# Memory attention chunk by chunk, output weights loaded by half rows beside it, gated values weighed two steps behind their load

## The chip, the cores and the metric

The kernel runs on one core of one Trainium2 chip. The metric is the device time of one execution in microseconds (us); less is better. The core has TensorE (PE, with its weight loads as PEld), VectorE (DVE), ScalarE (ACT), GpSimd (POOL) and SyncE (SP), which here only issues DMAs.

## What is computed

One decoder layer on x of 2048 x 1024, with a memory of 256 tokens, all in float32. Cut to what matters:

```python
h    = rmsnorm(x, norm_g)
proj = h @ w_in                               # 1024 -> 3584: q | k | v (768 each) | qm (256) | gate (1024)
mix  = dilated_window_mixer(q, k, v)          # 12 heads in 3 groups; each group's output is scaled by its
                                              # share of the groups' softmax denominators (per head and row)
mo   = memory_attention(qm, rmsnorm(mem, mem_norm_g), w_mem_kv)   # 4 heads over 256 memory tokens
y    = concat([mix, mo]) * silu(gate)         # 2048 x 1024
x    = x + y @ w_out                          # w_out 1024 x 1024
return rmsnorm(x, final_norm_g)
```

## The kernel before

**Tiling.** x is held transposed and split in two float32r parts, `xH` and `xL` (high and rest), as 4 chunks of 512 rows by 8 tiles of 128 columns (`k`). A projection of 128 columns for one chunk is 24 matmuls (8 tiles, three products high*high, high*rest, rest*high; L140 to L142). `Rb` holds the rows' 1/rms, 512 columns a chunk.

**Stages.** First six passes (three groups by two head pairs) with four chunks each do the window attention. Then comes the memory stage: eight units, one for each head pair `pp` and chunk `c`, pp outside and c inside. A unit is `proj_q`, `proj_gate` (48 matmuls) and a `burst`: the scores of this unit (`mem_scores`, L448), and the values (L437) of the unit two before it. Between a unit's scores and its values lie, for each half of the unit: row maxima (DVE L453), exponentials (ACT L457), reciprocals (DVE L460), a scaling of four tiles (POOL L464), a 32x32-block transpose (DVE L329) and a turn through DRAM (`turn_tiles`: one DMA of 512 KB out, L332, four of 128 KB back, L338). `values` ends with the product with the gate (DVE L420) and the store of the gated chunk to `z_dr` (SP L429).

Last comes the output stage: for each chunk `c` four blocks (`out_block`) of 48 matmuls (L642 to L644), `y` of that chunk by the output weights, then residual, RMS norm and the store. The residual rows are loaded at the start of a block (L633).

**What is prepared beside it.** `shares` turns the softmax statistics (six transposes on PE, L551, copies by DVE, 24 small DMAs to `st_dr`), computes the groups' shares and stores them to `f_dr`. `load_wo(k)` loads one full row tile of the output weights (512 KB) into a buffer of tag `wh`, casts it into `woH` (ACT L598) and subtracts into `woL` (POOL L599); `woH` and `woL` lie over chunks 0 and 1 of `xH` and `xL`. `make_y(c, k)` loads the gated values from `z_dr` (256 KB, L612) and for k < 6 their shares from `f_dr` (two of 128 KB, L616), multiplies (POOL, for every third k DVE; L618), casts into `yH` (ACT L619) and subtracts into `yL` (DVE L620); `yH` and `yL` of an even chunk lie over chunk 2 of `xH` and `xL`, of an odd one over chunk 3. Its shares' buffer is `wraw` with two buffers, which `load_w` uses too.

**What sets the order.** The projections and output blocks are generators; `run` counts a slot at each `yield` (every six matmuls; four slots a projection, eight a unit, eight a block), and `at(n, f)` calls f n slots later. So slots put the side work into program order. The framework then places the instructions on each engine by its own plan of when their operands are ready, with program order as the priority, so an engine's order can differ from the program's. All DMAs go through SP's one queue, in order: a DMA that waits holds up those behind it. With the slot M in which the memory stage begins: `shares` begins at M+13, the loads of weights 19 at M+16, the eight `load_wo` stand at M+41 to M+59, the eight `make_y(0, k)` at M+56 to M+63, the first output block at M+64.

Of the kernel before, what the change touches and what calls it, by code (L numbers as in the profile page):

```python
# [34 lines left out]
def trunk_kernel(ctx, tc, xT, xrows, w_in, g_in, w_out, memT, mrows, g_mem, w_mem, g_fin, nbias, ident_in, out):  # L35
# [78 lines left out]
    def to_blocks(ap, g):  # L114

        if g == 0:
            return ap.rearrange("p (b r i) -> p r b i", b=4, r=16)
        if g == 1:
            return ap.rearrange("p (b j i) -> p j b i", b=4, j=4)
        return ap  # L120

    def from_proj(ap, g):

        if g == 0:
            return ap.rearrange("p (r b i) -> p r b i", r=16, b=4)
        if g == 1:
            return ap.rearrange("p (j b i) -> p j b i", j=4, b=4)
        return ap
# [277 lines left out]
    def values(st, g, pp, c):  # L406
        o = pbank(ps_o, "po")
        for half in st["halves"]:
            assert half.ready
            if g == 3:  # L410
                mem_values(o, st, pp, half)
                continue
            for b in half.blocks:
                ts = [t for t in range(2) if (b, t, 0) in half.at]
                for t in ts:
                    for h in range(2):
                        pe.matmul(o[h * HD:(h + 1) * HD, b * P:(b + 1) * P], st["v"][:, b + t, h * HD:(h + 1) * HD],
                                  half.turned(b, t, h), start=(t == ts[0]), stop=(t == 1))
        u = st["u"]
        v.tensor_tensor(from_proj(u, g), from_proj(u, g), to_blocks(o, g), op=ALU.mult)  # L420
        dst = z_dr[g][:, pp, :]
        if g == 0:
            sp.dma_start(dst.rearrange("p (r c n) -> p r c n", r=16, c=4)[:, :, c, :],
                         u.rearrange("p (r n) -> p r n", r=16))
        elif g == 1:
            sp.dma_start(dst.rearrange("p (j r n) -> p j r n", j=4, r=4)[:, :, c, :],
                         u.rearrange("p (j n) -> p j n", j=4))
        else:
            sp.dma_start(dst[:, c * CH:(c + 1) * CH], u)  # L429
# [66 lines left out]
    def memory_kv(st):  # L496
        gm = sb([P, NK], F32, "gm", 1)
        sp.dma_start(gm, g_mem)
        halves = [t.bitcast(F32).rearrange("p k n -> p (k n)").rearrange("p (k n) -> p k n", k=4) for t in w_tiles()]
        for i, m in enumerate(halves):  # L500
            sp.dma_start(m, memT[:, 4 * i:4 * i + 4, :])
        yield
        rm = sb([P, 2, P], F32, "rm", 1)
        r = spread(rm, st["squares"], 2)
        next(r)
        for i, m in enumerate(halves):
            for j in range(2):
                for k in range(2 * j, 2 * j + 2):
                    a.activation(m[:, k, :], m[:, k, :], AF.Copy, scale=gm[:, 4 * i + k:4 * i + k + 1])
                yield  # L510
        next(r)
        raws = []

        def load(i):
            for j in range(2):
                raw = sb([P, 4, P], F32, "wraw", 2) if j else tmp().rearrange("p (k n) -> p k n", k=4)
                sp.dma_start(raw, w_mem[i, :, 4 * j:4 * j + 4, :])
                raws.append(raw)

        load(0)  # L520
        yield
        yield
        st["kk"] = sb([P, 5 * P], F32, "kk", 2)
        for i in range(4):
            if i < 3:
                load(i + 1)
            if i == 2:
                for _ in range(5):
                    yield
            ps = pbank()[:, :NMEM]  # L530
            for j in range(2):
                for k in range(4):
                    pe.matmul(ps, raws[2 * i + j][:, k, :], halves[j][:, k, :], start=(j + k == 0), stop=(j + k == 4))
                yield
            t = st["kk"][:, i * NMEM:(i + 1) * NMEM] if i < 2 else tmp()[:, :NMEM]
            v.tensor_tensor(t.rearrange("p (b n) -> p b n", b=2), ps.rearrange("p (b n) -> p b n", b=2), rm, op=ALU.mult)
            if i < 2:
                continue
            yield
            if i == 2:  # L540
                vb = sb([P, 5, P], F32, "vb", 2).rearrange("p b n -> p (b n)")[:, :2 * NMEM]
                st["v"] = vb.rearrange("p (k n) -> p k n", k=2)
            shift_tiles(st["v"][:, :, (i - 2) * P:(i - 1) * P], t.rearrange("p (k n) -> p k n", k=2))
        yield


    def shares():
        for i, src in enumerate((nm_all, l_all)):
            for g in range(3):
                pt = pbank()  # L550
                pe.transpose(pt[:64, :P], src[:, g].rearrange("p h b -> p (h b)"), ident)  # L551
                t = sb([P, CH], F32, "wraw", 2)[:64, :P]
                v.tensor_copy(t, pt[:64, :P])
                for h in range(4):
                    dst = st_dr[2 * g + i, h]
                    s = t[16 * h:16 * h + 16, :]
                    if g == 2:
                        sp.dma_start(dst.rearrange("(r n) -> r n", r=16), s)
                    elif g == 1:
                        sp.dma_start(dst.rearrange("(j b i) -> b j i", j=4, b=16),  # L560
                                     s.rearrange("b (j i) -> b j i", j=4))
                    else:
                        sp.dma_start(dst.rearrange("(r b i) -> b r i", r=16, b=16),
                                     s.rearrange("b (r i) -> b r i", r=16))
            yield
        q = S // 32
        m = sb([P, 5 * P], F32, "kk", 2)[:, :6 * q].rearrange("p (s n) -> p s n", s=6)
        sp.dma_start(m, st_dr.rearrange("s h (b n) -> (h b) s n", n=q))
        for _ in range(4):
            yield  # L570
        f = sb([P, 5, P], F32, "vb", 2).rearrange("p b n -> p (b n)")[:, :4 * q]
        f = f.rearrange("p (s n) -> p s n", s=4)
        v.tensor_tensor(f[:, 3, :], m[:, 0, :], m[:, 2, :], op=ALU.min)
        v.tensor_tensor(f[:, 3, :], f[:, 3, :], m[:, 4, :], op=ALU.min)
# [17 lines left out]
    def row_tile(tag):  # L592
        return sb([P, NK, P], F32R, tag, 4).bitcast(F32).rearrange("p k n -> p (k n)")

    def load_wo(k):
        raw = row_tile("wh")
        sp.dma_start(raw, w_out[:, k, :])
        a.copy(woH[:, k, :], raw)  # L598
        gp.tensor_tensor(woL[:, k, :], raw, woH[:, k, :].bitcast(F32), op=ALU.subtract)  # L599

    staged = []

    def make_y(c, k):
        yH, yL = xH[:, 2 + c % 2, k, :], xL[:, 2 + c % 2, k, :]
        cs = slice(c * CH, (c + 1) * CH)
        if not staged:
            kk = sb([P, 5 * P], F32, "kk", 2)
            vb = sb([P, 5, P], F32, "vb", 2).rearrange("p b n -> p (b n)")
            spare = row_tile("wl")
            staged.extend([kk[:, :CH], vb[:, :CH], spare[:, :CH], spare[:, CH:]])  # L610
        t = staged[k % 4]
        sp.dma_start(t, z_dr[k // 2][:, k % 2, cs])  # L612
        if k < 6:
            f = sb([P, CH], F32, "wraw", 2)
            for h in range(2):
                sp.dma_start(f[h * HD:(h + 1) * HD, :],  # L616
                             f_dr[k // 2, 2 * (k % 2) + h:2 * (k % 2) + h + 1, cs].broadcast_to([HD, CH]))
            (v if k % 3 == 2 else gp).tensor_tensor(t, t, f, op=ALU.mult)  # L618
        a.copy(yH, t)  # L619
        v.tensor_tensor(yL, t, yH.bitcast(F32), op=ALU.subtract)  # L620

    outr = out.rearrange("(u r) d -> r u d", r=16)
    gfin = []
# [52 lines left out]
    def at(delay, fn):  # L676
        todo.setdefault(slot[0] + delay, []).append(fn)
# [45 lines left out]
    for idx, (g, pp) in enumerate(pairs):  # L723
# [55 lines left out]
            burst((st, g, pp, c), 1, nbs[0])  # L779
            prev = st  # L780
        ws = following
    at(12, lambda: steps(shares()))
    for pp in range(2):
        for c in range(NC):
            st = {}
            if pp == 1 and c >= 1:
                for i, k in enumerate(((0, 1, 2), (3, 4, 5), (6, 7))[c - 1]):
                    at(2 * i + 1, lambda k=k: load_wo(k))
            if pp == 1 and c == 3:
                for k in range(NK):  # L790
                    at(k, lambda k=k: make_y(0, k))
            run(proj_q(st, 3, c, ws[2 + 2 * pp]))
            run(proj_gate(st, 3, c, ws[1 + 2 * pp], "nb" if (4 * pp + c) % 3 == 1 else "u"))
            if pp == 0 and c == 1:
                ws.append(load_w(w_in[19]))
            burst((st, 3, pp, c), 2)
    for c in range(NC):
        for b in range(4):
            if c < NC - 1:
                at(3, lambda: (make_y(c + 1, 2 * b), make_y(c + 1, 2 * b + 1)))  # L800
            run(out_block(c, b))
            if c == 0 and b in (0, 2):
                burst()
# [62 lines left out]
```

## Time and profile before

| | us |
|---|---|
| median of 3 runs | 1015.41 (1009.09 to 1016.02) |
| the profiled execution | 1015.06 |
| its span in the trace | 1013.3 |
| PE busy in the span | 968.4 (96%) |
| DVE, ACT, POOL busy | 425.3, 324.3, 257.1 |
| DMA: moved, share of 16 engines | 134.30 MB, 42.7% |

How to read it: a busy PE says that matmuls are in flight, also at a lowered clock; so beside the busy time stands the clock that was granted, as a share of 2.4 GHz (1.00 is 2.4 GHz, 0.50 is 1.2 GHz). Matmuls overlap, so their mean duration is longer than the distance from one start to the next. The memory stage lies at about 657 to 785 us of the span, the output stage behind it.

### The profile page before, as it was taken

How to read it: one execution, taken by the hardware profiler on the slowest of the kernel's cores; microseconds unless marked ns; L12 is line 12 of the kernel's file. 1: busy time of each engine (PE TensorE's matmuls, PEld its weight loads, DVE VectorE, ACT ScalarE, POOL GpSimd, SP SyncE). 2: the span in 40 equal slices, each digit the busy share in tenths (PEclk: the TensorE clock that was granted, in tenths of full speed). 3: DMA queues.
4: the chain of work that ended last, by engine and by line, in shares of the span. 5: the costliest groups of instructions: out<-in, count | busy, mean ns of one | idle time of the engine just before them, and what ended most of it. 6: DMA issues, size and time to landing. Idle time of an engine off the chain costs nothing. (4 is left out here: it accounts for less than half of the span.)

```text
span 1013.3 us, 13854 instructions
## 1 busy us (share of the span) xinstructions
PE 968.4 (96%) x4836; PEld 761.8 (75%) x4836; DVE 425.3 (42%) x982; ACT 324.3 (32%) x984; POOL 257.1 (25%) x396
## 2 busy tenths in 40 slices
PE   7899999999999999999999999999999679899997
PEld 5688888887788888777777777777767357688886
DVE  7866333333343333333333344324544434455433
ACT  5756422232234222432232324232333321222111
POOL 4411500140014000411132112143366641112000
PEclk9899999999999999999999999999999689899999
DMA  5465411142124322432245335414655777788311
GB/s 194 152 198 177 146 64 62 53 146 71 60 94 148 103 83 84 140 105 83 87 132 156 115 95 165 138 50 105 187 158 177 220 223 215 240 238 220 125 63 62
DMA packets 100982, 135.18 MB, mean 133 GB/s; under 512 B 29744, under 2 KB 63792, under 8 KB 100912
## 3 DMA queue, kind: packets, MB, share of 16 engines
q1 hardware_dynamic: 100912, 134.30, 42.7%
q8 instruction: 38, 0.62, 0.3%
q14 instruction: 32, 0.26, 0.1%
HBM read 89.14 MB, written 45.12 MB: 132 GB/s over the span
## 5 line engine op out<-in xcount | busy, mean ns | idle before, releaser
L140 PE MATMUL pp<-xH,wh 128*128 128x512 f32 x896 | 361.7, 404 | 3.2 <-DVE kk L249 2.8
L142 PE MATMUL pp<-xH,wl 128*128 128x512 f32 x896 | 357.7, 399 | 2.1 <-DVE wl L78 2.1
L141 PE MATMUL pp<-xL,wh 128*128 128x512 f32 x896 | 357.8, 399 | 1.4 <-DVE xL L198 1.4
L140 PEld LDWEIGHTS pp<-xH,wh 128*128 128x128 f32 x896 | 169.9, 190 | 53.4 <-issue 9.4
L142 PEld LDWEIGHTS pp<-xH,wl 128*128 128x128 f32 x896 | 169.7, 189 | 46.2 <-DVE wl L78 4.1
L141 PEld LDWEIGHTS pp<-xL,wh 128*128 128x128 f32 x896 | 169.9, 190 | 42.5 <-DVE xL L198 2.6
L320 POOL COPY vb<-mid 32x128 f32<-32x128 f32 (+1 forms) x208 | 59.6, 287 | 255.8 <-DVE mid L317 247.6
L642 PE MATMUL pp<-xH 128*128 128x512 f32 (+1 forms) x264 | 105.9, 401 | 16.0 <-ACT xH L619 11.9
L320 ACT COPY vb<-mid 32x128 f32<-32x128 f32 (+1 forms) x208 | 60.7, 292 | 166.7 <-DVE mid L317 164.4
L78 POOL TENSOR_TENSOR wl<-wraw,wh 128x512 fp32r<-128x512 f32 x52 | 67.5, 1312 | 151.3 <-ACT wh L77 146.0
L643 PE MATMUL pp<-xL,xH 128*128 128x512 f32 (+1 forms) x264 | 104.6, 397 | 0.0
L644 PE MATMUL pp<-xH,xL 128*128 128x512 f32 (+1 forms) x264 | 103.1, 395 | 0.0
L374 ACT ACTIVATE p<-p,nm_all 128x128 f32<-128x128 f32 (+1 forms) x192 | 86.1, 450 | 39.3 <-DVE nm_all L373 26.9
L329 DVE STREAM_TRANSPOSE mid<-p 128x1024 f32<-128x1024 f32 (+1 forms) x56 | 66.9, 1194 | 53.6 <-DMA t_dr<-mid 30.9
L464 POOL TENSOR_SCALAR p<-p,sm 128x256 f32<-128x256 f32 x64 | 59.4, 945 | 62.4 <-DVE sm L460 32.7
L642 PEld LDWEIGHTS pp<-xH 128*128 128x128 f32 x264 | 51.6, 196 | 29.8 <-ACT xH L619 14.0
L306 DVE SCALAR_TENSOR_TENSOR tmp<-pp,Rb 128x512 f32<-128x512 f32 x32 | 22.1, 690 | 123.6 <-PE pp L142 123.5
L307 ACT ACTIVATE u<-tmp 128x512 f32<-128x512 f32 x29 | 18.3, 631 | 140.3 <-DVE tmp L306 138.8
L373 DVE CUSTOM_DVE_ANT_0 p<-ps,nb 128x128 f32<-128x128 f32 (+1 forms) x192 | 57.0, 361 | 8.0 <-PE ps L395 7.9
L644 PEld LDWEIGHTS pp<-xH,xL 128*128 128x128 f32 x264 | 51.9, 197 | 10.8 <-DVE xL L620 0.2
L643 PEld LDWEIGHTS pp<-xL,xH 128*128 128x128 f32 x264 | 51.8, 196 | 10.1
L77 ACT CAST wh<-wraw 128x512 fp32r<-128x512 f32 (+1 forms) x60 | 33.9, 587 | 64.7 <-DMA wraw<-in_w_in 36.1
(129 smaller groups left out, 818.4 us busy)
## 6 DMA issues: line engine op xcount, KB each, us to landing
t_dr<-mid SPq DMA_DIRECT2D x46, 512.0 KB, 3.0
p<-t_dr SPq DMA_DIRECT2D x184, 128.0 KB, 3.5
wraw<-in_w_in SPq DMA_DIRECT2D x56, 256.0 KB, 3.0
wh<-in_xrows SPq DMA_DIRECT2D x16, 512.0 KB, 5.1
out<-wh SPq DMA_DIRECT2D x15, 512.0 KB, 2.7
z_dr<-u SPq DMA_DIRECT2D x29, 256.0 KB, 2.4
wraw<-f_dr SPq DMA_DIRECT2D x48, 128.0 KB, 5.2
tmp<-in_xT SPq DMA_DIRECT2D x22, 256.0 KB, 3.9
```

What stands on the lines that cost most here:

```text
L78: on.tensor_tensor(wl, raw, wh.bitcast(F32), op=ALU.subtract)
L140: pe.matmul(ps, wh[:, k, :], xh, start=(k == 0), stop=False)
L141: pe.matmul(ps, wh[:, k, :], xl, start=False, stop=False)
L142: pe.matmul(ps, wl[:, k, :], xh, start=False, stop=(k == NK - 1))
L320: (gp.tensor_copy if (i + j) % 2 else a.copy)(dst[32 * j:32 * j + 32, :, 32 * i:32 * i + 32], mid[32 * i:32 * i + 32, :, 32 * j:32 * j + 32])
L329: v.transpose(mid.rearrange("p (j t b) -> p t j b", j=4, t=n), src.rearrange("p (t j b) -> p t j b", t=n, j=4))
L373: v.tensor_tensor_reduce(p, sc, bias, -SCALE, BIG, ALU.add, ALU.min, nm)
L374: a.activation(p, p, AF.Exp, bias=nm, scale=-1.0, accum_out=l)
L464: gp.tensor_scalar(w, w, sm[:, 1, h, b:b + 1], None, op0=ALU.mult)
L642: pe.matmul(ps, yH[:, k, bs], woH[:, k, ns], start=(k == 0), stop=False)
L643: pe.matmul(ps, yH[:, k, bs], woL[:, k, ns], start=False, stop=False)
L644: pe.matmul(ps, yL[:, k, bs], woH[:, k, ns], start=False, stop=(k == NK - 1))
```

## The change

The eight units of the memory stage run in another order, (0,0), (0,1), (1,0), (1,1), (0,2), (1,2), (0,3), (1,3), so that chunks 0 and 1 are done with after four units. Then 16 half rows of the output weights (256 KB each) are loaded, one a slot from M+32, into four buffers (two in `Rb`, two of `wraw`), and each is split three slots after its load; every third subtraction goes to DVE. `make_y(0, k)` stands at M+52 to M+59, with four buffers for the values and three for the shares (partly in `Rb`), and its arithmetic (`finish`) is put two slots behind its loads; in the output stage the two `make_y` of a block stand at its slots 1 and 4, before both at 3. The store of the gated chunk is put two slots behind its product. `shares` begins at M+21 and keeps its copies in `vb` and `kk` rather than in `wraw`. Weights 19, which the third unit now needs at M+16, are loaded at M+13. No matmul is added or removed.

```diff
@@ -418,6 +418,9 @@
                                   half.turned(b, t, h), start=(t == ts[0]), stop=(t == 1))
         u = st["u"]
         v.tensor_tensor(from_proj(u, g), from_proj(u, g), to_blocks(o, g), op=ALU.mult)
+        at(2, lambda: store_z(u, g, pp, c))
+
+    def store_z(u, g, pp, c):
         dst = z_dr[g][:, pp, :]
         if g == 0:
             sp.dma_start(dst.rearrange("p (r c n) -> p r c n", r=16, c=4)[:, :, c, :],
@@ -542,14 +545,19 @@
                 st["v"] = vb.rearrange("p (k n) -> p k n", k=2)
             shift_tiles(st["v"][:, :, (i - 2) * P:(i - 1) * P], t.rearrange("p (k n) -> p k n", k=2))
         yield
+        yield
+        ws.append(load_w(w_in[19]))
+        yield
 
 
     def shares():
+        kk = sb([P, 5 * P], F32, "kk", 2)
+        vb = sb([P, 5, P], F32, "vb", 2)
         for i, src in enumerate((nm_all, l_all)):
             for g in range(3):
                 pt = pbank()
                 pe.transpose(pt[:64, :P], src[:, g].rearrange("p h b -> p (h b)"), ident)
-                t = sb([P, CH], F32, "wraw", 2)[:64, :P]
+                t = (vb[:64, 3 * i + g, :] if 3 * i + g < 5 else kk[:64, :P])
                 v.tensor_copy(t, pt[:64, :P])
                 for h in range(4):
                     dst = st_dr[2 * g + i, h]
@@ -564,11 +572,11 @@
                                      s.rearrange("b (r i) -> b r i", r=16))
             yield
         q = S // 32
-        m = sb([P, 5 * P], F32, "kk", 2)[:, :6 * q].rearrange("p (s n) -> p s n", s=6)
+        m = kk[:, :6 * q].rearrange("p (s n) -> p s n", s=6)
         sp.dma_start(m, st_dr.rearrange("s h (b n) -> (h b) s n", n=q))
         for _ in range(4):
             yield
-        f = sb([P, 5, P], F32, "vb", 2).rearrange("p b n -> p (b n)")[:, :4 * q]
+        f = vb.rearrange("p b n -> p (b n)")[:, :4 * q]
         f = f.rearrange("p (s n) -> p s n", s=4)
         v.tensor_tensor(f[:, 3, :], m[:, 0, :], m[:, 2, :], op=ALU.min)
         v.tensor_tensor(f[:, 3, :], f[:, 3, :], m[:, 4, :], op=ALU.min)
@@ -592,32 +600,43 @@
     def row_tile(tag):
         return sb([P, NK, P], F32R, tag, 4).bitcast(F32).rearrange("p k n -> p (k n)")
 
-    def load_wo(k):
-        raw = row_tile("wh")
-        sp.dma_start(raw, w_out[:, k, :])
-        a.copy(woH[:, k, :], raw)
-        gp.tensor_tensor(woL[:, k, :], raw, woH[:, k, :].bitcast(F32), op=ALU.subtract)
+    def load_wo(i):
+
+        k, ns = i // 2, slice(i % 2 * CH, i % 2 * CH + CH)
+        raw = Rb[:, ns] if i % 4 < 2 else sb([P, CH], F32, "wraw", 2)
+        sp.dma_start(raw, w_out[:, k, ns])
+
+        def split():
+            a.copy(woH[:, k, ns], raw)
+            (v if i % 3 == 2 else gp).tensor_tensor(woL[:, k, ns], raw, woH[:, k, ns].bitcast(F32), op=ALU.subtract)
+
+        at(3, split)
 
     staged = []
 
     def make_y(c, k):
+
         yH, yL = xH[:, 2 + c % 2, k, :], xL[:, 2 + c % 2, k, :]
         cs = slice(c * CH, (c + 1) * CH)
         if not staged:
             kk = sb([P, 5 * P], F32, "kk", 2)
             vb = sb([P, 5, P], F32, "vb", 2).rearrange("p b n -> p (b n)")
-            spare = row_tile("wl")
-            staged.extend([kk[:, :CH], vb[:, :CH], spare[:, :CH], spare[:, CH:]])
-        t = staged[k % 4]
+            staged.append([Rb[:, i * CH:(i + 1) * CH] for i in range(3)] + [vb[:, :CH]])
+            staged.append([sb([P, CH], F32, "wraw", 2), sb([P, CH], F32, "wraw", 2), kk[:, :CH]])
+        t, f = staged[0][k % 4], staged[1][k % 3]
         sp.dma_start(t, z_dr[k // 2][:, k % 2, cs])
         if k < 6:
-            f = sb([P, CH], F32, "wraw", 2)
             for h in range(2):
                 sp.dma_start(f[h * HD:(h + 1) * HD, :],
                              f_dr[k // 2, 2 * (k % 2) + h:2 * (k % 2) + h + 1, cs].broadcast_to([HD, CH]))
-            (v if k % 3 == 2 else gp).tensor_tensor(t, t, f, op=ALU.mult)
-        a.copy(yH, t)
-        v.tensor_tensor(yL, t, yH.bitcast(F32), op=ALU.subtract)
+
+        def finish():
+            if k < 6:
+                (v if k % 3 == 2 else gp).tensor_tensor(t, t, f, op=ALU.mult)
+            a.copy(yH, t)
+            v.tensor_tensor(yL, t, yH.bitcast(F32), op=ALU.subtract)
+
+        at(2, finish)
 
     outr = out.rearrange("(u r) d -> r u d", r=16)
     gfin = []
@@ -779,25 +798,23 @@
             burst((st, g, pp, c), 1, nbs[0])
             prev = st
         ws = following
-    at(12, lambda: steps(shares()))
-    for pp in range(2):
-        for c in range(NC):
-            st = {}
-            if pp == 1 and c >= 1:
-                for i, k in enumerate(((0, 1, 2), (3, 4, 5), (6, 7))[c - 1]):
-                    at(2 * i + 1, lambda k=k: load_wo(k))
-            if pp == 1 and c == 3:
-                for k in range(NK):
-                    at(k, lambda k=k: make_y(0, k))
-            run(proj_q(st, 3, c, ws[2 + 2 * pp]))
-            run(proj_gate(st, 3, c, ws[1 + 2 * pp], "nb" if (4 * pp + c) % 3 == 1 else "u"))
-            if pp == 0 and c == 1:
-                ws.append(load_w(w_in[19]))
-            burst((st, 3, pp, c), 2)
+    at(20, lambda: steps(shares()))
+    for n, (pp, c) in enumerate(((0, 0), (0, 1), (1, 0), (1, 1), (0, 2), (1, 2), (0, 3), (1, 3))):
+        st = {}
+        if n == 4:
+            for i in range(2 * NK):
+                at(i, lambda i=i: load_wo(i))
+        elif n == 6:
+            for k in range(NK):
+                at(4 + k, lambda k=k: make_y(0, k))
+        run(proj_q(st, 3, c, ws[2 + 2 * pp]))
+        run(proj_gate(st, 3, c, ws[1 + 2 * pp], "nb" if n % 3 == 1 else "u"))
+        burst((st, 3, pp, c), 2)
     for c in range(NC):
         for b in range(4):
             if c < NC - 1:
-                at(3, lambda: (make_y(c + 1, 2 * b), make_y(c + 1, 2 * b + 1)))
+                for i in range(2):
+                    at(1 + 3 * i, lambda k=2 * b + i: make_y(c + 1, k))
             run(out_block(c, b))
             if c == 0 and b in (0, 2):
                 burst()
```

## Rows read from the trace of the kernel before

**Rows 1.** Header, then busy time by stretch: us, engines' busy (x instructions), PEclk, DMA share, GB/s.

```profile
core 0 of [0], span 1013.3 us
685.00:690.00 5.00, 4.93 (x19) 3.49 (x21) 1.81 (x5) 0.00 (x0) 0.00 (x0) 0.66 0.41 118
690.00:785.00 95.00, 94.89 (x482) 68.94 (x480) 47.34 (x84) 30.03 (x95) 51.64 (x47) 1.00 0.53 160
785.00:830.00 45.00, 28.37 (x101) 18.83 (x100) 18.30 (x25) 14.69 (x43) 27.74 (x24) 0.73 0.69 218
785.00:880.00 95.00, 73.51 (x297) 53.27 (x296) 42.39 (x67) 24.14 (x59) 35.06 (x32) 0.84 0.75 225
880.00:1000.00 120.00, 120.00 (x531) 99.42 (x530) 51.89 (x98) 22.14 (x38) 17.07 (x19) 1.00 0.51 153
```

**Rows 2.** Who PE waited for, whole span: us in total, times, longest.

```profile
PE pp L642 <- ACT xH L619: 11.9, 4, 3.9
PE pp L642 <- DVE wh L647: 4.1, 2, 2.7
PE pp L551 <- DVE q L288: 3.3, 1, 3.3
```

**Rows 3.** PE's matmuls by line, 785 to 880 us: count, busy, mean ns, idle before.

```profile
L642 PE MATMUL pp<-xH 128*128 128x512 f32 x73 | 33.3, 456 | 16.0 <-ACT xH L619 11.9 <-DVE wh L647 4.1
L643 PE MATMUL pp<-xL,xH 128*128 128x512 f32 x71 | 31.3, 441 | 0.0
L644 PE MATMUL pp<-xH,xL 128*128 128x512 f32 x71 | 29.8, 435 | 0.0
L437 PE MATMUL po<-p,vb 128*64 128x256 f32 x64 | 9.7, 426 | 2.3 <-DMA p<-t_dr 2.3
L448 PE MATMUL ps<-kk,q 64*128 64x256 f32 x16 | 4.3, 549 | 3.2 <-ACT p L457 3.2
```

**Rows 4.** PE in order of time, memory stage: start, us, instructions.

```profile
705.94 2.00 PE L448 MATMUL ps<-kk,q 64*128 64x256 f32 x16
...
711.64 1.08 PE L437 MATMUL po<-p,vb 128*64 128x256 f32 x8
```

**Rows 5.** ACT in order of time, casts of y of chunk 0 (eight; first and last).

```profile
800.37 0.62 ACT L619 CAST xH<-kk 128x512 fp32r<-128x512 f32 x1 [5.18 <-POOL kk L618]
...
828.17 1.14 ACT L619 CAST xH<-wl 128x512 fp32r<-128x512 f32 x2
```

**Rows 6.** Who SP's queue waited for, 690 to 880 us: total, times, longest.

```profile
SPq L429 <- DVE u L420: 34.4, 5, 11.0
SPq L597 <- POOL xL L599: 11.7, 2, 11.5
```

**Rows 7.** POOL's instructions by line, 690 to 880 us: count, busy, mean ns, idle before.

```profile
L464 POOL TENSOR_SCALAR p<-p,sm 128x256 f32<-128x256 f32 x56 | 52.1, 948 | 60.5 <-DVE sm L460 32.7 <-issue 20.5 <-DMA wh<-in_w_out 4.6
...
L599 POOL TENSOR_TENSOR xL<-wh,xH 128x1024 fp32r<-128x1024 f32 x8 | 19.5, 2448 | 1.7 <-ACT xH L598 1.7
...
L78 POOL TENSOR_TENSOR wl<-wraw,wh 128x512 fp32r<-128x512 f32 x2 | 2.6, 1286 | 3.6 <-ACT wh L77 3.6
```

**Rows 8.** DMA, 690 to 880 us: packets, MB, share; then issues, KB each, us to landing.

```profile
q1 hardware_dynamic: 24928, 36.47, 63.7%
...
p<-t_dr SPq DMA_DIRECT2D x64, 128.0 KB, 3.8
t_dr<-mid SPq DMA_DIRECT2D x15, 512.0 KB, 3.7
wh<-in_w_out SPq DMA_DIRECT2D x8, 512.0 KB, 4.9
...
wraw<-in_w_in SPq DMA_DIRECT2D x2, 256.0 KB, 3.7
```

**Rows 9.** DVE, then POOL, in order of time: start, us; three single instructions.

```profile
782.78 0.72 DVE L308 SCALAR_TENSOR_TENSOR u<-u,tmp 128x512 f32<-128x512 f32 x1
...
802.50 2.44 DVE L308 SCALAR_TENSOR_TENSOR nb<-nb,tmp 128x512 f32<-128x512 f32 x1 [0.79 <-ACT nb L307]
...
802.01 2.37 POOL L599 TENSOR_TENSOR xL<-wh,xH 128x1024 fp32r<-128x1024 f32 x1 [1.67 <-ACT xH L598]
```

## The prediction

> **What bounds the kernel now.** I read the busy time by stretch first. From 690 to 785 us, the memory stage, and from 880 to 1000 us, most of the output stage, PE is busy all the time at a granted clock of 1.00: there the matmuls set the time, and no part of the change shortens them. Between, from 785 to 880 us, PE is busy 73.5 of 95 us at a mean clock of 0.84 [rows 1]. So what can be won lies at that seam.
>
> Next, how much it is. The matmuls of that stretch are listed by line [rows 3]: 73 + 71 + 71 = 215 of the output blocks, 64 of the values, 16 of the scores. At the pace of undisturbed stretches an output matmul takes 120 us / 531 = 0.226 us [rows 1], eight of the values 1.08 us and sixteen of the scores 2.00 us [rows 4]. That is 48.6 + 8.6 + 2.0 = 59.2 us of work in 95 us: 35.8 us are lost. Of these 95 - 73.5 = 21.5 us are idle, and 14.3 us are matmuls that ran at the lower clock after the gaps. So each idle us here cost 1.67 us in all, a ratio that I use below for idle time that stays or is new. Idle at 785 to 830 us are 45 - 28.4 = 16.6 us, behind it 4.9 us [rows 1]. By the same ratio I call the first share B, 27.7 us, and the second C, 8.2 us.
>
> Then, who PE waited for. The largest wait, 11.9 us, is of the first output matmul of a product on the cast of y [rows 2]. In ACT's order of time the eight casts of chunk 0 come from 800.4 to 829.3 us [rows 5], though the block that reads them could begin at about 785 us: y is late, and piecemeal, by up to 44 us. C is mainly the wait for the addition that frees a PSUM bank, 4.1 us [rows 2], which itself stands behind late loads. A third place is earlier: a transpose of the shares waited 3.3 us for the eviction of q [rows 2], and the 5 us behind it ran at 0.66, 4.93 x 0.34 = 1.7 us more [rows 1]. I call it A, 5.0 us.
>
> Last, why y is late. SP's queue stood 34.4 us at the store of gated chunks, waiting for their product, and 11.7 us at the loads of the output weights, waiting for POOL's subtraction to free one of their buffers [rows 6]. Whatever is behind them in the one queue, turns and loads of y too, stood as well. The DMA engines were busy only 0.53 of the time in the memory stage and 0.75 behind it [rows 1]. The transfers came late, not slowly.
>
> One more reading: a unit's values should by program order run ahead of the scores that follow them. But scores run at 705.9 us and the values of an earlier unit at 711.6 us [rows 4]. The order on an engine is a plan's, so a slot in the code is only about a place in time. I take a unit as 48 x 0.226 + 2.0 + 2 x 1.08 = 15 us and a slot without burst as 1.36 us.
>
> **The change, part by part.**
>
> *Order of the units.* The matmuls are the same. Weights 19 are needed at M+16 rather than M+32, and are loaded at M+13. Two loads of 3.7 us [rows 8], overlapping, two casts and two subtractions of 1.29 us on POOL [rows 7] are some 8 us against three slots and a burst, also 8 us; the buffers are free earlier, so the plan can start the load ahead of its slot. I take 0; with nothing but the three slots as cover it is 8 - 3 x 1.36 = 4 us.
>
> *Shares at M+21 with copies of their own.* The transposes now stand behind memory_kv's work, and their banks need not wait for `wraw`. But again they stand in a gate projection with q just finished. Bounds 0 to 5.0 us of A; I leave 1.0.
>
> *Output weights.* Before, eight loads from M+41 on, the last beside y. Now 16 halves at M+32 to M+47, all split by M+50. Work on POOL: 11 subtractions x 1.286 = 14.1 us, 5 go to DVE; before 8 x 2.45 = 19.6 us [rows 7]. With the scaling of two units, 16 x 0.948 = 15.2 us, POOL has 29.3 us to do in two units, 30 us. That is tight. DMA: 8 x 0.524 = 4.2 MB, and a unit moves 2 x 0.524 + 8 x 0.131 + 0.262 = 2.36 MB, so 8.9 MB in 30 us, 297 GB/s. What the engines do at full share, estimated from 36.47 MB in 190 us at 63.7%, is 301 GB/s [rows 8]. Tight again. The cover is the distance of two units, 30 us, between scores and values; the chain in it is eight scalings of 0.948, 7.6 us, and the turn's 3.7 and 3.8 us [rows 7, 8], 15 us, and with maxima, exponentials and transposes an estimated 20, so 10 us of slack. Bounds: 0 if the slack covers all, up to 7.5 us (below) if POOL doesn't keep up. I take 3 us idle, 5 us in all.
>
> *y of chunk 0 at M+52 rather than M+56, arithmetic two slots behind the load, seven buffers for six.* It no longer competes with three loads of the output weights and their subtractions. Moved by DMA between M+32 and M+64 are 4.2 + 8 x 0.262 + 6 x 0.262 + 4 x 2.36 = 17.3 MB, 57.5 us at 301 GB/s, where PE has 60. That needs 96%, and behind the memory stage 0.75 was reached [rows 1]. At 85%, between them, it is 67.6 us, y complete 7.6 us behind M+64. The first half of a block takes y tile by tile over 24 x 0.226 = 5.4 us, and values of the two last units can fill in; about half of the lateness shows. I take 4 us idle, 6.7 in all, of B's 27.7. Bounds 0 and 27.7.
>
> *Store two slots later; the two make_y of an output block apart, their arithmetic later.* These move the waits of 34.4 us [rows 6] off SP's head, and let an in-order ACT or DVE not stand at a load that was just issued. It is work beside PE, so what it gives is part of B and of C. Moved per make_y: three DMA issues (four buffers of values and three of shares keep them from blocking), one product, one cast, one subtraction. The residual rows and y of the next chunk still compete at the start of the output stage, so I take half of C, 4.1 us; bounds 0 and 8.2.
>
> **Sum.** To be won are A 5.0 + B 27.7 + C 8.2 = 40.9 us. Left over are 1.0 + 5.0 + 6.7 + 4.1 = 16.8 us. Gain 24.1 us: 1015.1 - 24.1 = 991.0 us for the profiled execution (its span 1013.3 us and 1.8 us around it), which is within 0.4 us of the median of the runs before.
>
> One rule of the Trainium skill speaks against the change. The trace has it this way: a DVE instruction with two SBUF inputs took 0.72 us alone, and 2.44 us where it began inside a POOL subtraction of 2.37 us [rows 9]. Five subtractions that move to DVE and two gates are seven such instructions beside a POOL that is nearly always busy; a wait of up to 1.29 us each is 9 us on a DVE that was busy 47 of 95 us [rows 1]. That changes no term, but it adds to the first rival. The Trainium skill, SBUF — State Buffer, section Who interferes with whom, says that only the port pair shared by DVE and GpSimd causes contention, and as an exclusive lock. By that rule whichever comes second stands for the whole instruction; the trace agrees (2.44 against 0.72 us).
>
> **The rivals.**
>
> *1. The jam moves into units five to eight.* For it: POOL with 29.3 of 30 us, DMA at 297 of 301 GB/s, DVE behind POOL. Against it: 10 us of slack for each unit. If POOL gets through at 85%, its 29.3 us take 34.5, 4.5 us idle, 7.5 in all; y is late by the full 7.6 us, 12.7 in all; C stays, 8.2; A leaves 1.0. Left over 29.4 us: 1003.6 us.
>
> *2. Slower: half loads stand at SP's head.* The queue stood 11.5 us once because a raw buffer was not free [rows 6]. Twelve of the 16 halves reuse one of four buffers, three rounds. If each stands as long, that is 34.5 us with the turns behind it; the slack of 10 us is used up once, 24.5 us idle are left, 41 us by the ratio: 991 + 41 = 1032 us. Slower than before from 24.1 / 1.67 = 14.4 us idle on. Against it: a half is 1.29 us on POOL for 2.45, and there were two buffers where now are four.
>
> *3. It does not do what it says: y is as late as before.* If the halves go one behind another, 16 x 3.7 = 59 us [rows 8], they fill the time up to the output stage, and y's loads queue behind them. For it: in this stretch half the bytes took 3.7 us where the whole row took 4.9 us [rows 8]. Then B and C stay, and only A is won but for 1 us: 1011 us. Against it: four buffers allow four in flight.
>
> **How the numbers follow.** Forecast, 991 us with 982 to 1001: 0.60. Nearly all of it won, 974 to 982 us: 0.07. Rival 1: 0.14. Rival 3: 0.13. Rival 2: 0.06. About 1% is what a measurement here can tell from no change, 1005.3 to 1025.6 us. Faster: 0.60 + 0.07 + 0.10 of rival 1 = 0.77. Same: the rest of rival 1 and 0.11 of rival 3, 0.15. Slower: rival 2 and the rest, 0.08. The range is 978 to 1008 us: it takes in the bounds of A, B and C but for a corner and all of rival 1, and leaves out rival 2 and most of rival 3.
>
> **What would show it.** Right: no wait of a transpose of the shares on q; casts of chunk 0's y done within 10 us of the first output matmul; PE idle around the seam under 12 us in place of 21.5; DMA share near 0.85 in the last four units; the last unit's projections done some 4 us earlier. Rival 1 shows PE idle with a lowered clock in the last four units, behind POOL's scalings or turns. Rival 2 shows SP waiting at L597's successor for tens of us. Rival 3 shows the casts still spread over 30 us. The forecast is wrong above all if PE waits for values of units five to eight, or if y's loads are issued later than planned.

## The result and the profile after

The changed kernel takes 1001.54 us (median, 999.95 to 1003.44), the kernel before 1013.62 us with one more run. The ratio is 0.989 with a 95% interval of 0.984 to 0.993: 12 us or 1.1% faster, about half of the 24 us forecast. The profiled execution took 1002.67 us, its span is 1000.9 us.

Busy time by stretch of the changed kernel (us, engines' busy with instructions, granted clock, DMA share, GB/s). The first row is the stretch behind the wait of the shares' transpose, the second the seam, the third the seam with the bounds of [rows 1], the last roughly the four later units of the memory stage.

```profile
700.00:705.00 5.00, 4.76 (x17) 3.50 (x17) 2.23 (x8) 0.00 (x0) 4.61 (x5) 0.66 0.39 116
780.00:860.00 80.00, 64.68 (x274) 46.35 (x273) 34.88 (x59) 19.33 (x52) 32.59 (x32) 0.89 0.79 236
785.00:880.00 95.00, 80.92 (x341) 60.33 (x342) 43.14 (x76) 23.73 (x59) 31.32 (x32) 0.91 0.79 238
...
715.00:780.00 65.00, 65.00 (x318) 46.83 (x317) 32.48 (x61) 21.58 (x67) 34.52 (x34) 1.00 0.57 180
```

Who PE waited for from 600 to 980 us (us in total, times, longest):

```profile
PE pp L661 <- DVE wh L666: 8.5, 3, 3.1
PE pp L559 <- DVE q L288: 3.8, 1, 3.8
PE ps L451 <- ACT p L460: 3.2, 2, 1.6
PE pp L661 <- ACT xH L636: 3.0, 2, 2.6
...
PE po L440 <- DMA p<-t_dr: 0.5, 1, 0.5
```

In this kernel the output matmuls are L661 to L663 (before L642 to L644), the addition that frees their bank is L666 (L647), the cast of y L636 (L619), the scores L451, the values L440, the shares' transposes L559 and POOL's scaling L467 (L464).

PE's matmuls by line at 780 to 860 us, which holds all of the seam's idle time:

```profile
L661 PE MATMUL pp<-xH 128*128 128x512 f32 x61 | 27.5, 451 | 11.5 <-DVE wh L666 8.5 <-ACT xH L636 3.0
L662 PE MATMUL pp<-xL,xH 128*128 128x512 f32 x61 | 26.0, 427 | 0.0
L663 PE MATMUL pp<-xH,xL 128*128 128x512 f32 x60 | 25.3, 432 | 0.0
L440 PE MATMUL po<-p,vb 128*64 128x256 f32 x64 | 8.7, 391 | 0.6 <-DMA p<-t_dr 0.5
L451 PE MATMUL ps<-kk,q 64*128 64x256 f32 x16 | 4.1, 532 | 3.2 <-ACT p L460 3.2
L141 PE MATMUL pp<-xL,wh 128*128 128x512 f32 x4 | 1.6, 394 | 0.0
```

Counted as in the prediction: 182 output matmuls of 0.226 us, 64 of the values at 1.08 us for eight, 16 scores in 2.0 us, and twelve matmuls of a projection (four on each of three lines, one shown) of about 0.23 us are 54.5 us of work in 80. Lost are 25.5 us, 15.3 of them idle. Before it was 35.8 and 21.5 us [rows 1, 3]. So the seam gave 35.8 - 25.5 = 10.3 us. The ratio of loss to idle time, 25.5 / 15.3 = 1.67, is the same as before.

Beside [rows 2] the waits say this: the wait on the cast of y fell from 11.9 to 3.0 us. The wait on the addition that frees a bank rose from 4.1 to 8.5 us. The wait of the shares' transpose stands, 3.8 us for 3.3, and so does the wait of the scores on exponentials, 3.2 us in both kernels [rows 3].

ACT's first and last cast of y of chunk 0 (start, us):

```profile
791.43 0.62 ACT L636 CAST xH<-Rb 128x512 fp32r<-128x512 f32 x1 [0.97 <-POOL Rb L635]
...
810.37 0.63 ACT L636 CAST xH<-vb 128x512 fp32r<-128x512 f32 x1
```

They span 19.6 us, before 28.9 us [rows 5]. y is still late, but less so, and PE's idle time now mostly ends with another wait, that for an addition.

### The profile page after: what moved, and what is told of

It is laid out like the page before. It is cut to its first block, busy times and chain, and to the rows that moved or that the text cites. A ratio compares the mean times of both kernels' runs of the same rounds, so it can differ in the third digit from the quotient of the medians.

```text
span 1000.9 us, 13892 instructions
## 1 busy us (share of the span) xinstructions
PE 962.5 (96%) x4836; PEld 757.9 (76%) x4836; DVE 420.7 (42%) x987; ACT 324.6 (32%) x992; POOL 253.8 (25%) x399
## 4 chain that ended last, share of the span: by engine, by line
PE 86%; issue 3%; DMA 3%; DVE 3%; POOL 2%; ACT 1%; SPq 1%; POOLq 0%; DVEq 0%; ACTq 0%
PE pp L140 20%; PE pp L142 20%; PE pp L141 20%; PE pp L661 5%; PE pp L663 5%; PE pp L662 5%; PE ps L395 4%; PE po L417 3%; POOL p L467 1%; PE ps L451 1%; PE po L440 1%; PE pp L536 1%; DMA wh<-in_xrows 1%; DMA wraw<-in_w_in 1%; DVE xL L198 1%
## 5 line engine op out<-in xcount | busy, mean ns | idle before, releaser
L320 POOL COPY vb<-mid 32x128 f32<-32x128 f32 (+1 forms) x208 | 60.1, 289 | 254.3 <-DVE mid L317 246.1
L661 PE MATMUL pp<-xH 128*128 128x512 f32 (+1 forms) x264 | 104.8, 397 | 11.5 <-DVE wh L666 8.5
L320 ACT COPY vb<-mid 32x128 f32<-32x128 f32 (+1 forms) x208 | 60.7, 292 | 166.7 <-DVE mid L317 164.5
L663 PE MATMUL pp<-xH,xL 128*128 128x512 f32 (+1 forms) x264 | 103.0, 393 | 0.0
L467 POOL TENSOR_SCALAR p<-p,sm 128x256 f32<-128x256 f32 x64 | 60.8, 969 | 59.0 <-DVE sm L463 31.6
L661 PEld LDWEIGHTS pp<-xH 128*128 128x128 f32 x264 | 51.1, 194 | 25.6 <-DVE wh L666 9.9
L663 PEld LDWEIGHTS pp<-xH,xL 128*128 128x128 f32 x264 | 51.0, 193 | 10.9 <-DVE xL L637 0.6
```

What stands on the lines that cost most here:

```text
L320: (gp.tensor_copy if (i + j) % 2 else a.copy)(dst[32 * j:32 * j + 32, :, 32 * i:32 * i + 32], mid[32 * i:32 * i + 32, :, 32 * j:32 * j + 32])
L467: gp.tensor_scalar(w, w, sm[:, 1, h, b:b + 1], None, op0=ALU.mult)
L661: pe.matmul(ps, yH[:, k, bs], woH[:, k, ns], start=(k == 0), stop=False)
L663: pe.matmul(ps, yL[:, k, bs], woH[:, k, ns], start=False, stop=(k == NK - 1))
```

## The experiments

Each ratio is to the kernel before on the same chip, with its 95% interval; the changed kernel's is 0.989 [0.984, 0.993]. Against it a difference under some 0.005 can't be told. Each diff is against the changed kernel, but for the last.

My theory after the result: half of the gain is missing because A (the shares) was not won, C (the additions) grew, and y, though planned earlier, still stands on SP's queue.

**y of chunk 0 four slots later, as before (e3_ylate)**

```diff
-                at(4 + k, lambda k=k: make_y(0, k))
+                at(8 + k, lambda k=k: make_y(0, k))
```

> y of chunk 0 is made at M+56 to M+63, as before the change, instead of M+52; all else as in the changed kernel. Theory (its loads come when SP's queue gets to them, behind a store and turns that wait, so their place in the program is worth little): within 2 us of 1001.5, 1000 to 1004 us. Rival (the early place is what the change won): four slots later, 5.4 us idle by 1.67, 9 us, 1010 us.

Measured: 1012.25 us, ratio 0.996 [0.994, 0.998], 7.4 us worse than the changed kernel by the ratios, with some 5 us of uncertainty. The rival holds: the early place is most of what the change won. PE's waits show it, on the cast 11.1 us, about as before the change:

```profile
PE pp L661 <- ACT xH L636: 11.1, 4, 4.7
PE pp L661 <- DVE wh L666: 5.1, 2, 3.1
```

**y another four slots earlier (e7_yearly)**

```diff
-                at(4 + k, lambda k=k: make_y(0, k))
+                at(k, lambda k=k: make_y(0, k))
```

> make_y of chunk 0 another four slots earlier, M+48 to M+55; all else as in the changed kernel. e3_ylate, four slots later, lost 7.4 us (ratio 0.996 for 0.9887). Theory (earliness of y in the program is what pays, and it isn't used up): casts of chunk 0 done some 5 us earlier, ratio 0.982 to 0.985. Rival (what is left behind the seam are other waits, the additions and SP's queue behind the output weights): ratio 0.987 to 0.99.

Measured: 1002.94 us, ratio 0.987 [0.985, 0.989]; no gain that can be told. The waits on additions are 9.0 us, those on casts 3.7 us. The first cast of chunk 0 begins 4.6 us earlier than in the changed kernel (786.8 us for 791.4), but the last is done only 2 us earlier (809.0 for 811.0). What an earlier place gives is used up at M+52, and most of what is left is the additions.

**Arithmetic of y right behind its loads (e4_now)**

```diff
-        at(2, finish)
+        finish()
```

> The arithmetic of y stands right behind its loads again, not two slots later; all else as in the changed kernel. Theory A (the two steps keep ACT and DVE, which work in order, from standing at loads still on their way; that is a large part of the gain): half of the 12 us lost again, 1007 us or more, with longer waits of casts and scores. Theory B (the plan places the arithmetic by when it believes operands to be ready, so two slots in the program are nothing): 1000 to 1003 us.

Measured: 1004.15 us, ratio 0.988 [0.986, 0.991]. Theory B holds: the two steps of the arithmetic by themselves are worth nothing that shows. The waits are those of the changed kernel (8.0 us on additions, 2.6 us on casts).

**y's loads from ACT's queue (e6_actq)**

```diff
-        sp.dma_start(t, z_dr[k // 2][:, k % 2, cs])
+        a.dma_start(t, z_dr[k // 2][:, k % 2, cs])
...
-                sp.dma_start(f[h * HD:(h + 1) * HD, :],
+                a.dma_start(f[h * HD:(h + 1) * HD, :],
```

> The loads of make_y (gated values and shares) are issued from ACT's queue instead of SP's; all else as in the changed kernel, where the first of them is issued at 782.8 us, behind a store that stood 6.3 us and eight turns, though planned some 25 us ahead of the first output matmul. Theory (SP's queue in order is what makes y late): casts of chunk 0 begin 10 us earlier, waits on casts gone, ratio to before 0.98. Rival 1 (the DMA engines or POOL bound y, whatever the queue): ratio 0.987 to 0.99. Rival 2 (ACT, in order, now stands at the loads' buffers with the exponentials behind it): slower than the changed kernel, 0.99 to 1.0.

Measured: 1022.03 us, ratio 1.006 [1.004, 1.008], 17 us worse than the changed kernel. ACT's casts show that SP's queue had held the first tiles, and that freeing these alone gains nothing. The first two casts of chunk 0 come 32 and 30 us earlier than in the changed kernel, but the third only at 793.5 us, and the eighth is done at 810.4 us, in the changed kernel at 811.0:

```profile
759.44 0.62 ACT L636 CAST xH<-Rb 128x512 fp32r<-128x512 f32 x1 [1.36 <-DVE Rb L635]
766.57 0.62 ACT L636 CAST xH<-Rb 128x512 fp32r<-128x512 f32 x1 [6.51 <-DMA Rb<-z_dr]
...
793.51 0.62 ACT L636 CAST xH<-Rb 128x512 fp32r<-128x512 f32 x1 [2.01 <-POOL Rb L635]
```

PE waited 7.5 us once for a cast and 20.7 us in three waits for additions:

```profile
PE pp L661 <- DVE wh L666: 20.7, 3, 7.8
PE pp L661 <- ACT xH L636: 7.5, 1, 7.5
```

The time is worse than even rival 2 had it. Why the additions are late stands in DVE's order. Before each of the three waits DVE stands for a load of shares (into `kk`) that a multiplication of y needs (L635), 6.1, 8.0 and 5.7 us, and the additions come behind it. Around the first of them:

```profile
835.95 0.69 DVE L635 TENSOR_TENSOR Rb<-Rb,kk 128x512 f32<-128x512 f32 x1 [6.08 <-DMA kk<-f_dr]
...
837.22 1.28 DVE L666 TENSOR_TENSOR wh<-pp,wh 128x512 f32<-128x512 f32 x2
```

In the changed kernel DVE stood 6.0 us for such loads at 780 to 900 us, here 19.8. ACT too stands 21.1 us in one wait, before the squares of a block (L674), but it needs that block's addition and so comes behind it. The second addition also stood 4.3 us for its residual rows. Why the loads of shares come later from ACT's queue is not separated. My theory that SP's queue alone makes y late falls.

**Seven banks for the output blocks (e2_banks7)**

```diff
-            ps = pbank()[:, :hi - lo]
+            ps = (pbank(ps_s, "ps") if i else pbank())[:, :hi - lo]
```

> The second half of each output block accumulates in one of the four banks that the scores no longer need, so the output stage has seven banks instead of three; all else as in the changed kernel, where output matmuls wait 8.5 us in three waits for the addition that frees a bank. Theory (the additions stand in DVE's order behind the product with the gate and a transpose, which themselves wait for PE's values; with more banks PE needn't wait for them): the three waits are gone, 8.5 x 1.67 = 14 us, 987 us. Rival (the residual rows are late, or y is, and PE only waits somewhere else): 998 to 1002 us.

Measured: 999.44 us, ratio 0.984 [0.981, 0.987], 5 us better than the changed kernel. Alone that is at the edge of the noise; e10_best below confirms it. PE's waits from 785 us on:

```profile
PE pp L661 <- ACT xH L636: 6.0, 4, 2.4
PE ps L451 <- ACT p L460: 3.2, 2, 1.6
PE ps L661 <- ACT p L460: 1.6, 1, 1.6
```

The waits on additions are gone, so it was too few banks that PE waited for. The 14 us priced were not won: 4.6 us of idle time came up in place of the 8.5, 3.0 more on casts of y and 1.6 on a bank that the last scores still held. Of the 6.0 us on casts only 0.9 are on y of chunk 0; 2.7 are on that of chunk 1 (at 855 and 860 us) and 2.4 on that of chunk 2 (at 906 us), which in the changed kernel come to no wait. Why the additions are late can be read in the changed kernel. DVE in order of time around the first of the three waits:

```profile
818.61 0.69 DVE L420 TENSOR_TENSOR u<-u,po 128x512 f32<-128x512 f32 x1 [6.28 <-PE po L440]
819.21 1.24 DVE L329 STREAM_TRANSPOSE mid<-p 128x1024 f32<-128x1024 f32 x1
820.62 0.18 DVE L463 RECIPROCAL sm<-sm 128x4 f32<-128x4 f32 x1 [0.17 <-ACT p L460]
820.71 1.25 DVE L666 TENSOR_TENSOR wh<-pp,wh 128x512 f32<-128x512 f32 x2
```

DVE stood 6.3 us for PE's values, with the additions behind the product and the block transpose in its order. PE issued the values, ran out of banks and waited 2.9 us for the work that its values had held up. Before the other two waits DVE stood the same way, 5.5 and 3.7 us. The kernel before has it too, ahead of the first of its two waits on additions:

```profile
848.22 0.69 DVE L420 TENSOR_TENSOR u<-u,po 128x512 f32<-128x512 f32 x1 [6.20 <-PE po L437]
```

**The shares' transposes into one bank (e1_onebank), and all three ahead of their copies (e5_tfirst)**

```diff
+            bank = pbank()
             for g in range(3):
-                pt = pbank()
+                pt = bank[:, g * P:(g + 1) * P]
                 pe.transpose(pt[:64, :P], src[:, g].rearrange("p h b -> p (h b)"), ident)
```

> The three transposes of the shares in one step go into one PSUM bank instead of three; all else as in the changed kernel, whose trace still shows a transpose waiting 3.8 us for the eviction of q and 1.6 us of slow matmuls behind it. Theory (the transposes want banks that the projections hold): the wait is gone, 1001.5 - 5.4 = 996 us. Rival (DVE is late there whoever asks, and the next projection meets the same late eviction): a projection waits in place of the transpose, 1000 to 1002 us.

Measured: 1004.19 us, ratio 0.988 [0.986, 0.990]; the wait is 3.7 us, now on DVE's copy of the first transpose. This did not tell the theories apart, since the second transpose writes the bank that the copy still reads.

```diff
+            bank = pbank()
             for g in range(3):
-                pt = pbank()
-                pe.transpose(pt[:64, :P], src[:, g].rearrange("p h b -> p (h b)"), ident)
+                pe.transpose(bank[:64, g * P:(g + 1) * P], src[:, g].rearrange("p h b -> p (h b)"), ident)
+            for g in range(3):
+                pt = bank[:, g * P:(g + 1) * P]
```

> As e1_onebank, the three transposes of a step share one PSUM bank, but all three stand ahead of the three copies, so none writes a bank that a copy still reads; all else as in the changed kernel. In e1_onebank the second transpose waited 3.7 us for DVE's copy of the first, which stood in DVE's order behind a block transpose that waited 3.75 us for POOL's scaling. Theory (the place is lost only because PE's transposes depend on DVE there): the wait is gone, some 5 us less than the changed kernel, ratio to before 0.984. Rival (PE has run into DVE's hold-up anyway, and a projection waits for its bank): ratio 0.988 to 0.989, with a wait of a projection of 3 us in its place.

Measured: 1002.44 us, ratio 0.987 [0.985, 0.990]; no difference from the changed kernel that can be told. The wait shrank to 2.2 us and is now that of the second step's transposes. So banks are a smaller part, and DVE is late whoever asks. DVE and POOL of the changed kernel there:

```profile
698.30 1.25 DVE L329 STREAM_TRANSPOSE mid<-p 128x1024 f32<-128x1024 f32 x1 [3.75 <-POOL p L467]
699.47 0.13 DVE L463 RECIPROCAL sm<-sm 128x4 f32<-128x4 f32 x1
699.52 0.66 DVE L288 SCALAR_TENSOR_TENSOR q<-pp,Rb 128x512 f32<-128x512 f32 x1
...
694.65 3.62 POOL L467 TENSOR_SCALAR p<-p,sm 128x256 f32<-128x256 f32 x4 [9.62 <-DMA z_dr<-u]
```

The eviction of q (L288) stands in DVE's order behind a block transpose that stands 3.75 us for four scalings on POOL. POOL began them as soon as DVE's reciprocals (L463, at 694.37 us) were there, so the store in its brackets is not what it waited for last.

**Half of the scalings on DVE (e9_scale)**

```diff
-                    gp.tensor_scalar(w, w, sm[:, 1, h, b:b + 1], None, op0=ALU.mult)
+                    (v if h else gp).tensor_scalar(w, w, sm[:, 1, h, b:b + 1], None, op0=ALU.mult)
```

> Half of the scalings of the memory weights go from POOL to DVE (two of four in each half unit); all else as in the changed kernel. Theory (POOL's 3.6 us of scalings for each half unit hold up DVE's block transposes, and behind them evictions, turns and in the end y): the chain of a unit is some 3 us shorter, the 3.8 us wait of the shares' transpose shrinks, and the output weights are split earlier; ratio to before 0.982 to 0.985. Rival (DVE gets as much more as POOL gets less, and the hold-up is where DVE waits for ACT or DMA): 0.987 to 0.99.

Measured: 998.28 us, ratio 0.983 [0.981, 0.985]. The wait of the shares' transpose is gone; PE was busy all of the 30 us around it at full clock, in the changed kernel 26.2 us at 0.94:

```profile
685.00:715.00 30.00, 30.00 (x162) 22.71 (x158) 20.57 (x41) 9.96 (x36) 9.06 (x9) 1.00 0.52 139
```

A scaling took 0.46 us on DVE and 1.03 us on POOL, and the block transpose there stood 1.24 us for POOL instead of 3.75:

```profile
689.54 0.18 DVE L463 RECIPROCAL sm<-sm 128x4 f32<-128x4 f32 x1 [0.25 <-ACT p L460]
...
691.83 1.25 DVE L329 STREAM_TRANSPOSE mid<-p 128x1024 f32<-128x1024 f32 x1 [1.24 <-POOL p L467]
```

So A goes with the scalings, and not with the place of the shares. Not all of it is that the scalings are shorter: the reciprocals now also come 5.1 us ahead of the first transpose of the shares, in the changed kernel 1.8 us, so the plan's order has moved too. The two parts are not separated. At the seam the waits on additions stay, 8.9 us.

**All subtractions of the output weights on POOL (e11_allpool)**

```diff
-            (v if i % 3 == 2 else gp).tensor_tensor(woL[:, k, ns], raw, woH[:, k, ns].bitcast(F32), op=ALU.subtract)
+            gp.tensor_tensor(woL[:, k, ns], raw, woH[:, k, ns].bitcast(F32), op=ALU.subtract)
```

> All 16 subtractions of the output weights on POOL, none on DVE; all else as in the changed kernel. Theory (POOL's scalings and subtractions together are what is late in units five to eight, 29.3 us of some 30): 5 x 1.28 = 6.4 us more on POOL show in part, ratio to before 0.990 to 0.995. Rival (POOL has slack there): 0.987 to 0.989.

Measured: 1003.66 us, ratio 0.987 [0.985, 0.989], no difference that can be told. 6.4 us more on POOL there cost nothing that shows. So POOL's amount of work is not the limit in the later units; with e9_scale it is rather a scaling in front of a waiting DVE that costs.

**Both findings together (e10_best), and all scalings on DVE (e13_best2)**

The first has the edits of e2_banks7 and e9_scale. The second is the same with `v.tensor_scalar` for every scaling, not for half of them.

> Both findings together: seven banks in the output stage (e2_banks7) and half of the scalings on DVE (e9_scale); all else as in the changed kernel. Theory (two different waits, the shares' transpose behind POOL's scalings and the additions that free banks): the gains add, 0.9887 - 0.005 - 0.006 = ratio to before 0.978. Rival (both only move the seam's waits to the same late y): no better than e9_scale, 0.983.

> As e10_best, but all scalings on DVE, 0.46 us each for POOL's 1.0; POOL keeps the subtractions and products. Theory (POOL in front of DVE's block transposes is the hold-up in each unit): 0.975 to 0.978. Rival (DVE, 11.7 us more in 190 us with half of them and as much again here, now holds up its own evictions and the additions): 0.980 or more.

Measured: 991.35 us, ratio 0.976 [0.973, 0.978], and 993.68 us, ratio 0.977 [0.976, 0.979]. The gains add up, and the rest of the scalings give no more. Each edit is clear of the noise on top of the other: 0.976 for 0.983 with half of the scalings alone, and for 0.984 with seven banks alone. The first kernel is clearly faster than both the kernel before and the changed one. Its seam begins earlier, so it takes four stretches to hold it. They have 1.7 + 3.7 + 2.6 + 2.9 = 10.9 us idle, where the changed kernel has 15.3:

```profile
715.00:780.00 65.00, 63.29 (x309) 44.99 (x308) 39.17 (x74) 23.40 (x75) 26.98 (x24) 1.00 0.59 185
780.00:830.00 50.00, 46.31 (x207) 34.65 (x204) 22.57 (x38) 13.24 (x37) 15.88 (x14) 0.97 0.71 224
830.00:870.00 40.00, 37.40 (x163) 27.62 (x162) 20.57 (x40) 8.66 (x15) 6.00 (x7) 0.96 0.75 226
870.00:970.00 100.00, 97.14 (x420) 79.62 (x420) 46.23 (x86) 19.34 (x34) 15.51 (x16) 0.98 0.53 173
```

**The kernel before with half of the scalings on DVE (e12_bscale)**

```diff
-                    gp.tensor_scalar(w, w, sm[:, 1, h, b:b + 1], None, op0=ALU.mult)
+                    (v if h else gp).tensor_scalar(w, w, sm[:, 1, h, b:b + 1], None, op0=ALU.mult)
```

> The kernel before, with half of the scalings on DVE and nothing else. Theory (POOL's scalings held up A, the shares' transpose, in the kernel before too, and its subtractions of whole rows the seam): A is gone, 5 us, and the seam a little shorter, ratio 0.985 to 0.993. Rival (before the change SP's queue and the late place of y hide whatever POOL wins): 0.995 to 1.0.

Measured: 1003.93 us, ratio 0.989 [0.986, 0.991], as much as the whole change won. A is gone here too (PE is busy 29.73 us at 685 to 715 us, at a clock of 1.00). This seam too begins before 785 us; from 780 us on it is idle 15.4 + 3.7 = 19.1 us for 21.5, at a higher clock than in [rows 1]:

```profile
780.00:830.00 50.00, 34.62 (x146) 24.17 (x145) 28.43 (x43) 17.10 (x47) 22.90 (x18) 0.90 0.81 249
830.00:870.00 40.00, 36.32 (x164) 27.35 (x163) 18.74 (x36) 7.06 (x12) 4.22 (x5) 0.96 0.78 232
```

So the 12 us are A's 5.0 and, at the seam, 2.4 us less idle time and faster matmuls.

## Why the prediction was right in part

**What held.** The reading of the profile: the loss lies at the seam and in the shares, in all some 41 us, and the late y of chunk 0 is the largest part. The early place of y is what paid (7.4 us, shown by e3_ylate). y's residue was forecast at 4 us idle and measured at 3.0 us. The ratio of 1.67 between loss and idle time came out the same in the changed kernel.

**What came out by luck.** The later units were forecast with 3 us idle because POOL or the DMA would not keep up, and 3.7 us were measured, but of another kind. 3.2 of them are the last scores' wait on exponentials, and 0.5 the last values' wait on a turn; the kernel before had both, 3.2 and 2.3 us [rows 3]. Those 5.5 us I had counted into B and C as if y or the additions made them. Nor could a block begin at about 785 us: the last scores hold PE until 797.3 us in the kernel before, so its y was late by up to 32 us and not 44.

**A, forecast to leave 1.0 us, left 5.4 us** (3.8 idle, and 4.76 x 0.34 = 1.6 of slow matmuls). The step that failed is in the part on the shares: I read "the transpose waits for the eviction of q" as a matter of their place and buffers. One step further back in the trace the eviction stood behind a block transpose that stood for POOL: in the changed kernel 3.75 us for four scalings, in the kernel before 6.1 us for copies (L320) that stood behind eight scalings. Scalings come in every unit, so a move by eight slots met them again. e9_scale removes the wait by moving scalings alone, and e12_bscale does so in the kernel before.

**C, forecast to leave 4.1 us, grew to 14.2 us** (8.5 x 1.67). The step that failed is the half that I took off because stores and arithmetic move apart. The two steps of the arithmetic are worth nothing that shows (e4_now; the store alone was not tried). I had put the wait down to late loads, and it is mainly for banks: e2_banks7 takes it away with loads as they were. In the kernel before, late residual rows held one of the two additions for 1.2 us. That C grew because PE, with y earlier, came to the next limit sooner and stood there longer is argued, not shown; e3_ylate, with y late again, has 5.1 us of it for 8.5.

**The sum with the measured terms.** 5.4 + 3.7 x 1.67 + 3.0 x 1.67 + 14.2 = 30.8 us left over, not 16.8 (it is the 25.5 us of the seam and A counted by waits): 1015.1 - 40.9 + 30.8 = 1005.0 us. The profiled execution took 1002.7; the 2.3 us between have no single place in the trace and are within the spread of the runs.

**The expected tightness did not come.** DMA was to be near 0.85 and POOL full in the last four units. DMA was at 0.57, POOL busy 34.5 of 65 us, and PE lost nothing there. The plan stretched the 16 half loads over 88 us of SP's time. Eight go into `wraw`, the first and the last of all among them:

```profile
L607 SPq DMA_DIRECT2D wraw<-in_w_out x8: 328/340/937, 681.5 to 769.7; - x8
```

My sums of bytes over two units assumed that the slots of the program are times. The same error hid that y's first load would be issued only at 782.8 us, behind eight loads of turns, seven of them here:

```profile
777.96 4.78 SPq L338 DMA_DIRECT2D p<-t_dr  x7
782.78 0.43 SPq L627 DMA_DIRECT2D Rb<-z_dr  x1
```

**The rivals.** Rival 1's time, 1003.6 us, came close, but not its mechanism: PE lost nothing from 715 to 780 us, and more work on POOL there changed nothing that shows (e11_allpool). Rival 2 did not show: SP stood 12.7 us in four waits at the loads of the output weights, and PE had no wait there. Rival 3 did not show; y came earlier. The signs that I had named to look for told of the shortfall: a transpose of the shares still waits on q, the casts are done 18.5 us behind the first output matmul at 792.5 us where I wanted 10, the idle time is 15.3 us where I wanted under 12, and the last projection's last matmuls come 2.6 us earlier (782.3 us for 784.9) where I wanted 4.

**What stays open.** Whether the order of the units or the half rows pay by themselves was not separated; both make room for y at M+52. The worth of the store's two steps was not measured. Why y of chunk 0 stays late however early it stands in the program was not found: neither an earlier slot (e7_yearly) nor another queue (e6_actq) had the last cast done more than 2 us earlier.

## What to carry to other kernels

A wait names the last link; before pricing its removal, follow the in-order engine that is named one step further back, and ask what stands in front of it there. When you shorten the wait that ends last, price the next one behind it by the same trace. Here that was the wait for PSUM banks, which an addition was to free that itself stood behind other work: it took both edits on top of the change to win 24 us. And where a framework plans the order, a slot in the program is a priority and not a time, so sums of bytes over slots say little.

## What the runs showed of the hardware

The same scaling of 128x256 float32 in SBUF took 0.46 us on DVE and 0.95 to 1.03 us on POOL, and moving half of them off POOL (28 x 0.948 = 26.6 us of its time by [rows 7]) was worth 12 us in the kernel before (e12_bscale), in which POOL is busy a quarter of the time. An engine that is mostly idle cost time because it stood in a chain.

The same transfers from another engine's queue made a kernel 17 us slower than the changed one (e6_actq): the first tile of y was cast 32 us earlier, but PE then waited 20.7 us for additions instead of 8.5, behind a DVE that stood 19.8 us for loads of shares. Why those came later was not separated.
